# A two-layer conditioned trunk with a mixture of experts: additions of the rows read back placed further back, more PSUM banks for one-hot products, and two gating copies taken out

## The chip, the cores and the metric

The kernel runs on one core of one Trainium2 chip. The metric is the device time of one execution in microseconds (us). Before the change the median of three runs is 1160.93 us (1160.9 to 1163.3).

## What is computed

The reference runs two layers (DEPTH = 2) over 512 tokens of 1024 values. Each layer has a token mixer (three kinds of heads between an input and an output projection), and then a hierarchical mixture of experts: every token goes to 2 of 32 experts. The change lies in the second half:

```python
h = rms_norm(x, g_norm2[l]) * (1.0 + sc2) + sh2
x = x + ga2 * hier_moe(h, w_rg[l], b_rg[l], w_re[l], b_re[l], w1[l], w3[l], w2[l])
...
for g in range(N_GROUPS):                    # 4 groups of 8 experts, hidden width 256
    hid = jax.nn.silu(jnp.einsum('td,edf->tef', t, w1[g])) * jnp.einsum('td,edf->tef', t, w3[g])
    hid = hid * combine[:, g, :, None].astype(hid.dtype)   # zero but for a token's two experts
    y = y + jnp.einsum('tef,efd->td', hid, w2[g]).astype(jnp.float32)
```

## The kernel before

Everything is in float32; X is the running sum, four tiles of 128 tokens by 1024 (m = 0 to 3), kept in SBUF. SBUF is cut into 25 units of 1 MB (128 x 2048 values) that are handed out and given back in a queue.

**Experts in pairs.** The mixture runs over 16 pairs of experts. An expert's weights are three units: w1 and w3 by halves ("wg", two units, each loaded by two DMAs of 512 KB) and w2 (one unit, one DMA of 1024 KB), so a pair takes six units, 6 MB. Eighteen units hold weights, so up to three pairs are in SBUF. `pump` issues loads on SyncE's queue (SP), in order, as long as units are free; `refill` calls it again after a pair has released units. A DMA on that queue also waits until the one eight places before it has landed.

**One pair** (`pair(pr, b)`, b = pr % 2): the rows of up to 64 tokens of each of the two experts are gathered from DRAM (`gather`, an indirect DMA of GpSimd's queue, POOL) into xg, transposed (`rows_T`), multiplied with w1 and w3 (`stage1`, 32 records of L1118), made into the hidden values `hid` (ScalarE L1122, VectorE L1123), transposed (`hidden_T`, L1130 and L1131) and multiplied with w2 (`down`, L1138, two PSUM banks n = 0, 1). `extra` repeats this behind a branch when an expert has more than 64 tokens; it is taken at pair 0 and one later pair of layer 0, and at one pair of layer 1.

**Two ways back into X.** For pairs 0 to 12 `gated` multiplies with ga2 (L1153) and scatters the rows to y_d in DRAM. For the last three pairs (DIRECT = 3) the rows never leave the chip: `gated` (L1150) keeps them, `split` makes of them a high part yh (ScalarE L299) and a low part yl (VectorE L300), and `combine` adds them to X by a one-hot product: VectorE writes the 128 x 512 one-hot matrix `oh` (L1158), TensorE multiplies it with yh and yl into a PSUM bank per half tile (L1164, L1165), VectorE adds the bank to X (L1166). `combine` returns four steps, one per tile m; those of pair pr run inside `stage1` of pair pr + 1, after j = 2, 4, 6 and at its end; those of pair 15 run last of all. What was scattered is read back once (`fetch_back`, eight DMAs of 512 KB in pair 13) and added to X by `add_back(m)`, two VectorE additions of 128 x 1024 (L1208) per tile, in the tile order TAIL = (3, 0, 2, 1).

**Order.** In the last three pairs the order of TensorE, ScalarE, VectorE and GpSimd is that of the code (`manual_schedule(IN_LAST)`), before that only TensorE's and ScalarE's; SP is always in the order of the code. What belongs to the next layer (`front`) is placed between by a scheduler. Each engine works its own list in order, so an instruction that waits holds up all that stands behind it.

**The gate.** At the start of the mixture two gathers are issued, for pair 1 (xg[1]) and for the extra block of pair 0 (xg[2]). Then SP copies one value of each into a scrap of DRAM (L1218); since SP works in order, no load behind these copies starts before both gathers have landed. Behind them stand the two w2 loads of pair 2, and then everything from pair 3 on.

## Time and profile before

| | before |
|---|---|
| median of three runs | 1160.93 us |
| the profiled execution | 1162.47 us |
| its span, first to last instruction | 1160.5 us |
| TensorE busy | 1055.9 us (91%) |
| VectorE busy | 581.8 us (50%) |
| mean granted TensorE clock | 0.972 of full |

The mixture of layer 0 runs from about 318 to 602 us, that of layer 1 from about 880 us to the end. The page's 40 slices show the DMA engines 90% busy or more through most of both. Rows of a timeline are: start, duration, engine, line, operation, out<-in, tile, count, and in brackets how long the engine stood idle before and what ended it.

### The profile page before, as it was taken

The page shows a single profiled execution, that of the slowest core. Times are in us where ns is not written, and L with a number is a line of the kernel's source. Part 1 is how long each engine was busy: PE and PEld are TensorE (multiplying, and loading weights), DVE is VectorE, ACT ScalarE, POOL GpSimd, SP SyncE. Part 2 cuts the span into 40 slices and gives each one's busy share as a digit, 9 for nine tenths or more (in the row PEclk, how much of TensorE's full clock was granted, in tenths as well). Part 3 has the DMA queues.
Part 4 walks back from the last instruction along what each step waited for, and adds up shares of the span by engine and source line. Part 5 has one row for each costly group of instructions (what it writes and reads, how often), then busy time and mean ns, then how long its engine had stood idle before and what let it go on. Part 6 is the DMA issues. An engine that isn't in the chain of part 4 may idle for free. (4 is left out here: it accounts for less than half of the span.)

```text
span 1160.5 us, 15065 instructions
## 1 busy us (share of the span) xinstructions
PE 1055.9 (91%) x5152; PEld 571.9 (49%) x5152; DVE 581.8 (50%) x1315; ACT 359.4 (31%) x904; POOL 297.1 (26%) x260
## 2 busy tenths in 40 slices
PE   4999999999889999989779999999988998997975
PEld 1567666577533333333346676667763332332332
DVE  3567756778622222213584776587764221221255
ACT  2333354565311111201143333467632120120110
POOL 5655531002222221211134455110022221121100
PEclk9899999999999999999889999999989999999988
DMA  9957436816859999999976535620677999999992
GB/s 377 400 218 254 149 125 208 309 51 240 307 179 408 409 406 402 395 398 400 384 273 254 197 131 188 211 80 2 206 275 263 411 406 408 389 398 399 399 371 76
DMA packets 90909, 329.42 MB, mean 284 GB/s; under 512 B 19128, under 2 KB 23416, under 8 KB 76160
## 3 DMA queue, kind: packets, MB, share of 16 engines
q1 hardware_dynamic: 74992, 307.86, 69.6%
q0 software_dynamic: 14896, 17.50, 4.6%
q10 hardware_dynamic: 864, 2.17, 0.5%
q8 instruction: 74, 1.21, 0.4%
q14 instruction: 83, 0.68, 0.2%
HBM read 338.87 MB, written 29.93 MB: 318 GB/s over the span
## 5 line engine op out<-in xcount | busy, mean ns | idle before, releaser
L1118 PE MATMUL ps<-unit,unit 128*64 128x512 f32 x1120 | 271.5, 609 | 15.5 <-DMA unit<-w 14.8
L303 PE MATMUL ps<-unit,unit 128*128 128x512 f32 x448 | 182.6, 413 | 0.9 <-ACT unit L299 0.9
L304 PE MATMUL ps<-unit,unit 128*128 128x512 f32 x448 | 177.4, 397 | 2.8 <-POOL unit L300 1.5
L1118 PEld LDWEIGHTS ps<-unit,unit 128*64 128x64 f32 x1120 | 85.6, 140 | 186.0 <-issue 175.5
L305 PE MATMUL ps<-unit,unit 128*128 128x512 f32 x448 | 176.4, 396 | 0.5 <-DVE unit L300 0.5
L1138 PE MATMUL ps<-unit,unit 128*64 128x512 f32 x560 | 138.9, 618 | 6.5 <-ACT unit L1131 4.6
L1123 DVE SCALAR_TENSOR_TENSOR unit<-ps,slot_f,unit 128x256 f32<-128x256 f32 x35 | 16.9, 484 | 233.5 <-ACT unit L1122 233.5
L300 POOL TENSOR_TENSOR unit<-unit,unit 128x1024 fp32r<-128x1024 f32 (+1 forms) x46 | 104.9, 2284 | 100.9 <-ACT unit L299 100.9
L1122 ACT ACTIVATE unit<-ps 128x256 f32<-128x256 f32 x35 | 13.5, 384 | 371.5 <-issue 285.8
L299 ACT ACTIVATE unit<-unit 128x1024 fp32r<-128x1024 f32 (+1 forms) x92 | 87.9, 962 | 116.5 <-PE ps L305 60.8
L1087 POOL DMA_INDIRECT unit<-xn_d,slot_i x62 | 62.8, 1013 | 220.6 <-PEq L1186 160.9
L303 PEld LDWEIGHTS ps<-unit,unit 128*128 128x128 f32 x448 | 84.6, 189 | 36.6 <-issue 17.2
L304 PEld LDWEIGHTS ps<-unit,unit 128*128 128x128 f32 x448 | 84.9, 190 | 22.4 <-DVE unit L300 3.5
L305 PEld LDWEIGHTS ps<-unit,unit 128*128 128x128 f32 x448 | 84.3, 189 | 19.4 <-DVE unit L300 1.2
L1138 PEld LDWEIGHTS ps<-unit,unit 128*64 128x64 f32 x560 | 36.1, 139 | 82.8 <-issue 46.9
L1153 DVE TENSOR_TENSOR unit<-ps,unit 128x512 f32<-128x512 f32 x58 | 40.1, 692 | 72.1 <-PE ps L1138 72.1
L1092 POOL DMA_INDIRECT y_d<-unit,slot_y x29 | 29.6, 1021 | 171.2 <-DVE unit L1153 96.2
L535 ACT ACTIVATE unit<-unit,sm 128x512 f32<-128x512 f32 (+3 forms) x96 | 53.2, 555 | 32.9 <-DVE sm L533 32.4
L311 ACT ACTIVATE unit<-ps 128x512 f32<-128x512 f32 (+3 forms) x84 | 40.6, 490 | 70.6 <-PE ps L305 22.9
L1107 DVE TENSOR_SCALAR unit<-ps,cols 128x128 f32<-128x128 f32 x132 | 45.1, 404 | 31.4 <-PE ps L1098 31.1
L300 DVE TENSOR_TENSOR unit<-unit,unit 128x1024 fp32r<-128x1024 f32 (+1 forms) x46 | 54.9, 1198 | 11.7 <-ACT unit L299 11.1
L309 DVE COPY unit<-ps 128x512 f32<-128x512 f32 (+3 forms) x80 | 43.8, 552 | 31.8 <-PE ps L524 12.3
(223 smaller groups left out, 1346.0 us busy)
## 6 DMA issues: line engine op xcount, KB each, us to landing
unit<-w SPq DMA_DIRECT2D x256, 512.0 KB, 13.3
unit<-w SPq DMA_DIRECT2D x64, 1024.0 KB, 13.2
unit<-w_mod SPq DMA_DIRECT2D x48, 1024.0 KB, 7.0
unit<-w_in SPq DMA_DIRECT2D x16, 1024.0 KB, 14.9
y_d<-k_zero SPq DMA_DIRECT2D x16, 512.0 KB, 10.3
unit<-w_out SPq DMA_DIRECT2D x8, 1024.0 KB, 4.9
unit<-y_d SPq DMA_DIRECT2D x16, 512.0 KB, 10.7
unit<-w_in SPq DMA_DIRECT2D x8, 512.0 KB, 4.7
```

The costliest lines, as they stand in the source:

```text
L299: nc.scalar.activation(hi.bitcast(F32R), src, AF.Copy)
L300: (eng or nc.gpsimd).tensor_tensor(lo.bitcast(F32R), src, hi, op=OP.subtract)
L303: nc.tensor.matmul(o, ahi.bitcast(F32R), bhi.bitcast(F32R), start=first, stop=False)
L304: nc.tensor.matmul(o, ahi.bitcast(F32R), blo.bitcast(F32R), start=False, stop=False)
L305: nc.tensor.matmul(o, alo.bitcast(F32R), bhi.bitcast(F32R), start=False, stop=last)
L309: nc.vector.tensor_copy(dst, src)
L311: nc.scalar.activation(dst, src, AF.Copy)
L535: nc.scalar.activation(dst[:, :n], dst[:, :n], AF.Exp, bias=mx, scale=-1.0, accum_out=z)
L1087: nc.gpsimd.indirect_dma_start(out=dst, out_offset=None, in_=xn_d, in_offset=bass.IndirectOffsetOnAxis(ap=idx, axis=0), bounds_check=S - 1 ...
L1107: nc.vector.tensor_scalar(dst[:, j, :], p, cols[:, SC2, j:j + 1], cols[:, SH2, j:j + 1], op0=OP.mult, op1=OP.add)
L1118: nc.tensor.matmul(ph[64 * r:64 * r + 64, :], xT[:, j, 64 * r:64 * r + 64], ws[:, j % 4], start=j == 0, stop=j == 7, tile_position=(0, 64 ...
L1138: nc.tensor.matmul(PS[banks[n]][64 * r:64 * r + 64, :], hidT[b][:, j, 64 * r:64 * r + 64], w2[r][:, j, n, :], start=j == 0, stop=j == 1, t ...
```

## The change

It does three things. The two gate copies and their tile are taken out. In pair 15 the additions of the rows read back move: two tiles from the end of pair 14 into the second and third step of `combine` inside `stage1` of pair 15, the other two behind the one-hot matrix of the last `combine`, whose matrix is now written before `down` of pair 15 instead of after it. And the one-hot products inside `stage1` of pairs 14 and 15 use 4 and 6 PSUM banks instead of 2.

```diff
-    gate = dramp.tile([2, 1], F32, name="gate")
...
         TAIL = (3, 0, 2, 1)
+        tail = []
...
         gather(xg[2], slot_i[:, 0, 1:2])
-        for i, t in enumerate(xg[1:]):
-            nc.sync.dma_start(gate[i:i + 1, :], t[0:1, 0:1])
         pump()
 
         def pair(pr, b):
             tc.mark_branch_hint_location(f"extra{l}_{pr}", hint="LikelyTaken", engines=[mybir.EngineType.PE])
-            steps = combine(1 - b, slot_f[:, 0, pr - 1, 0:1], (6, 7)) if pr and direct(pr - 1) else []
+            steps = combine(1 - b, slot_f[:, 0, pr - 1, 0:1], (6, 7, 2, 3, 4, 5)[:6 if pr == 15 else 4]) if pr and direct(pr - 1) else []
             if pr == 15:
-                steps[1] = lambda s=steps[1]: (s(), add_back(TAIL[2]))
+                for k in (1, 2):
+                    steps[k] = lambda s=steps[k], m=TAIL[k - 1]: (s(), add_back(m))
             stage1(pr, b, xgT[b], slot_f[:, 1, pr, 0:1], steps)
...
                 hidden_T(b)
-                add_back(TAIL[3])
+                tail.extend(combine(b, slot_f[:, 0, pr, 0:1], (6, 7, 0, 4, 5, 1), done))
+                for m in TAIL[2:]:
+                    add_back(m)
             down(pr, b, each=lambda n: gated(pr, b, slot_y[:, pr, 0:1], n))
...
             refill(pr)
-            if pr == 14:
-                add_back(TAIL[0])
-                add_back(TAIL[1])
...
-            for f in combine(1, slot_f[:, 0, 15, 0:1], (6, 7, 0, 4, 5, 1), done):
+            for f in tail:
                 f()
```

VectorE, layer 1, from the end of pair 14 through `stage1` of pair 15 (unit_1 and unit_2 hold X; unit_339 and unit_336 are rows read back, tiles 3 and 0). Before:

```order
L300 TENSOR_TENSOR unit_335_10811<-ps_142,unit_334_10810 128x512
L1150 TENSOR_TENSOR ps_143<-ps_143,unit_3_172 128x512
L300 TENSOR_TENSOR unit_335_10811<-ps_143,unit_334_10810 128x512
L1208 TENSOR_TENSOR unit_2_171<-unit_2_171,unit_339_10815 128x1024 x2
L1208 TENSOR_TENSOR unit_1_170<-unit_1_170,unit_336_10812 128x1024 x2
L1158 TENSOR_SCALAR oh<-unit_3_172,slot_f 128x512
L1166 TENSOR_TENSOR unit_1_170<-unit_1_170,ps_146 128x512
```

After (line numbers are one or two lower):

```order
L299 TENSOR_TENSOR unit_335_10806<-ps_143,unit_334_10805 128x512
L1157 TENSOR_SCALAR oh<-unit_3_172,slot_f 128x512
L1165 TENSOR_TENSOR unit_1_170<-unit_1_170,ps_146 128x512
L1165 TENSOR_TENSOR unit_1_170<-unit_1_170,ps_147 128x512
L1165 TENSOR_TENSOR unit_1_170<-unit_1_170,ps_142 128x512
L1165 TENSOR_TENSOR unit_1_170<-unit_1_170,ps_143 128x512
L1208 TENSOR_TENSOR unit_2_171<-unit_2_171,unit_339_10810 128x1024 x2
L1165 TENSOR_TENSOR unit_2_171<-unit_2_171,ps_144 128x512
L1165 TENSOR_TENSOR unit_2_171<-unit_2_171,ps_145 128x512
L1208 TENSOR_TENSOR unit_1_170<-unit_1_170,unit_336_10807 128x1024 x2
L1122 SCALAR_TENSOR_TENSOR unit_258_8076<-ps_141,slot_f,unit_3_172 128x256
```

The matrix `oh` now stands right behind the last split; the four additions stand behind the additions of two products, and the last of them stands ahead of the hidden values (L1122).

VectorE, layer 0, behind the branch of pair 15, where the scheduler has placed work of layer 1's `front` (unit_195 receives lam_a and b_mod; unit_196 and unit_183 are a part of w_in). Before:

```order
L1208 TENSOR_TENSOR unit_1_170<-unit_1_170,unit_174_5155 128x1024 x2
L1150 TENSOR_TENSOR ps_142<-ps_142,unit_3_172 128x512
L300 TENSOR_TENSOR unit_172_5153<-ps_142,unit_171_5152 128x512
L1150 TENSOR_TENSOR ps_143<-ps_143,unit_3_172 128x512
L387 SCALAR_TENSOR_TENSOR unit_194_6001,lamt<-unit_195_6002 128x64 x2
L300 TENSOR_TENSOR unit_196_6003<-unit_183_5938,unit_196_6003 128x1024
L300 TENSOR_TENSOR unit_172_5153<-ps_143,unit_171_5152 128x512
L1158 TENSOR_SCALAR oh<-unit_3_172,slot_f 128x512
```

After:

```order
L1157 TENSOR_SCALAR oh<-unit_3_172,slot_f 128x512
L1208 TENSOR_TENSOR unit_2_171<-unit_2_171,unit_175_5153 128x1024
L250 MEMSET unit_195_5999 128x512
L1208 TENSOR_TENSOR unit_2_171<-unit_2_171,unit_175_5153 128x1024
L1208 TENSOR_TENSOR unit_1_170<-unit_1_170,unit_174_5152 128x1024
L250 MEMSET unit_195_5999 128x512
L1208 TENSOR_TENSOR unit_1_170<-unit_1_170,unit_174_5152 128x1024
L1149 TENSOR_TENSOR ps_142<-ps_142,unit_3_172 128x512
L386 SCALAR_TENSOR_TENSOR unit_194_5998,lamt<-unit_195_5999 128x64 x2
L299 TENSOR_TENSOR unit_196_6000<-unit_183_5933,unit_196_6000 128x1024
L299 TENSOR_TENSOR unit_172_5150<-ps_142,unit_171_5149 128x512
L1149 TENSOR_TENSOR ps_143<-ps_143,unit_3_172 128x512
```

Four additions and two memsets stand ahead of the first half of `gated` (L1149 on ps_142), and the two steps that read lam_a (L386) now stand between it and the split of that half.

GpSimd, layer 0, the loads of layer 1's small tables around the branch of pair 15. Before, ahead of the branch:

```order
L320 DMA unit_195_6002<-gk_a 128x64
L320 DMA unit_195_6002<-gq_a 128x64
L320 DMA unit_195_6002<-gq_c 128x64
L320 DMA unit_195_6002<-gk_c 128x64
L320 DMA unit_195_6002<-lam_a 128x256
L252 DMA unit_195_6002<-b_mod 4x512 x2
L1181 TENSOR_LOAD nblk
```

After, behind the branch:

```order
L319 DMA unit_195_5999<-lam_a 128x256
L408 DMA unit_189_5993<-k_rope 128x512
L373 DMA unit_189_5993<-k_band 128x1536
L251 DMA unit_195_5999<-b_mod 4x512
L379 TENSOR_TENSOR unit_198_6002<-unit_189_5993,unit_195_5999 128x256
```

The load of lam_a has moved from ahead of the branch to behind it; gk_a, gq_a, gq_c and gk_c stay ahead. All of them write into the unit that held the rows read back for tile 0, so they wait for `add_back(0)`.

## Rows read from the trace of the kernel before

**Rows 1.** The page's first line: span of the profiled execution.
```profile
span 1160.5 us, 15065 instructions
```
**Rows 2.** What SP's queue waited for, layer 1, 888 to 1112: us, times, longest.
```profile
SPq L158 <- DMA unit<-w: 159.0, 116, 3.6
```
**Rows 3.** The same view, layer 0, 340 to 566 us.
```profile
SPq L158 <- PEq L1188: 11.4, 1, 11.4
```
**Rows 4.** TensorE's timeline, layer 1, inside the mixture.
```profile
981.27 5.34 PE L1118 MATMUL ps<-unit,unit 128*64 128x512 f32 x14 [1.95 <-DMA unit<-w]
```
**Rows 5.** SP's timeline, layer 1, at the gate.
```profile
887.52 0.60 SPq L1218 DMA_DIRECT2D gate<-unit x2
888.23 24.97 SPq L158 DMA_DIRECT2D unit<-w  x19
```
**Rows 6.** Windows: stretch, length, busy by engine, clock, DMA share, GB/s; layer 1.
```profile
880.00:882.00 2.00, 2.00 (x11) 0.73 (x11) 2.00 (x10) 1.98 (x6) 0.00 (x0) 1.00 0.70 287
882.00:884.00 2.00, 2.00 (x12) 0.72 (x10) 0.20 (x1) 0.46 (x1) 1.00 (x1) 1.00 0.00 0
...
892.00:896.00 4.00, 4.00 (x20) 1.29 (x18) 1.34 (x2) 0.00 (x0) 1.31 (x2) 1.00 1.00 387
```
**Rows 7.** TensorE's timeline, layer 1, start of the mixture.
```profile
879.48 0.94 PE L1051 MATMUL ps<-unit 128*128 128x384 f32 x4
880.35 7.09 PE L1118 MATMUL ps<-unit,unit 128*64 128x512 f32 x32
...
893.45 7.04 PE L1118 MATMUL ps<-unit,unit 128*64 128x512 f32 x32
```
**Rows 8.** TensorE's timeline, layer 0, extra block of pair 0.
```profile
326.59 1.16 PE L1098 MATMUL ps<-ident,unit 128*128 128x128 f32 x8 [1.38 <-DMA unit<-xn_d,slot_i]
```
**Rows 9.** GpSimd's timeline, layer 0: issue of that block's gather.
```profile
322.26 1.02 POOL L1087 DMA_INDIRECT unit<-xn_d,slot_i  x1 [0.30 <-issue]
```
**Rows 10.** The gathers' line: issue to landing over all 62.
```profile
DMA to landing us min/median/max: 3.2/7.6/10.0
```
**Rows 11.** VectorE's timeline, layer 1, pairs 14 and 15.
```profile
1118.79 0.69 DVE L300 TENSOR_TENSOR unit<-ps,unit 128x512 fp32r<-128x512 f32 x1 [0.72 <-ACT unit L299]
1120.22 5.07 DVE L1208 TENSOR_TENSOR unit<-unit,unit 128x1024 f32<-128x1024 f32 x4 [0.74 <-DMA unit<-y_d]
...
1145.17 0.70 DVE L1150 TENSOR_TENSOR ps<-ps,unit 128x512 f32<-128x512 f32 x1 [4.71 <-PE ps L1138]
...
1148.85 0.69 DVE L300 TENSOR_TENSOR unit<-ps,unit 128x512 fp32r<-128x512 f32 x1 [0.72 <-ACT unit L299]
...
1153.01 3.68 DVE L1166 TENSOR_TENSOR unit<-unit,ps 128x512 f32<-128x512 f32 x6 [0.17 <-PE ps L1165]
```
**Rows 12.** TensorE's timeline, layer 1, pair 15.
```profile
1125.84 0.77 PE L1164 MATMUL ps<-unit,oh 128*128 128x512 f32 x1 [6.25 <-DVE oh L1158]
...
1130.24 0.49 PE L1164 MATMUL ps<-unit,oh 128*128 128x512 f32 x1
...
1133.24 0.50 PE L1164 MATMUL ps<-unit,oh 128*128 128x512 f32 x1
...
1140.20 0.46 PE L1130 MATMUL ps<-ident,unit 128*128 128x128 f32 x1 [3.34 <-PEq L1186]
```
**Rows 13.** Windows, layer 1, pair 15; the clock is the third number from the end.
```profile
1123.00:1128.00 5.00, 2.17 (x6) 1.35 (x8) 3.33 (x5) 0.00 (x0) 0.00 (x0) 0.50 1.00 411
```
**Rows 14.** VectorE's timeline, layer 0, pairs 14 and 15.
```profile
567.12 0.69 DVE L300 TENSOR_TENSOR unit<-ps,unit 128x512 fp32r<-128x512 f32 x1 [0.72 <-ACT unit L299]
...
593.60 0.68 DVE L300 TENSOR_TENSOR unit<-ps,unit 128x512 fp32r<-128x512 f32 x1
594.20 0.50 DVE L1158 TENSOR_SCALAR oh<-unit,slot_f 128x512 fp32r<-128x512 f32 x1
```
**Rows 15.** DMA issues by transfer: count, KB each, us to landing.
```profile
unit<-lam_a POOLq DMA_DIRECT2D x1, 128.0 KB, 8.7
unit<-gk_a POOLq DMA_DIRECT2D x1, 32.0 KB, 6.0
```

## The prediction

> **What bounds the kernel now.** The span is 1160.5 us [rows 1]; the profiled execution took 1162.47 us, 1.5 us above the median of the runs shown (1160.93). I make the sum in the span's time and take it off the median. The change touches three places, and I read each by what ends the waits there.
>
> First, the mixture of layer 1. From 888 to 1112 us SP's queue waits 159 us in 116 pieces for an earlier weight load to land, and for hardly anything else [rows 2]: the loads run back to back, and no wait for a free unit is visible beside that. TensorE waits for weights in the pairs of that stretch ([rows 4] is one of seven such stalls). So from 888 us on, the stream of weights sets the time, and a stream that is ahead by some microseconds ends the stage as much earlier. Second, the start of this stream: SP stands at the gate until 887.52 and issues the two w2 loads of pair 2 at 888.23 [rows 5], while the DMA engines are idle: their work runs out inside 880 to 882, and from 882 to 884 they move nothing [rows 6]. Third, the end of layer 1: after the last split of pair 14 VectorE makes four additions, 5.07 us, behind a wait of 0.74 us for the rows read back [rows 11], and only then the one-hot matrix; TensorE stands idle for 6.25 us for it [rows 12].
>
> Layer 0 has the same code and other limits. At its start SP stands 11.4 us for the end of pair 0's extra block [rows 3], whose weights' units it needs; the two w2 loads lie ahead of that wait either way. At its end the scheduler has woven in work of layer 1.
>
> **Layer 1, gate out: -5.8 us.** Removed are two small DMAs; moved are two loads of 1024 KB and, behind them, the whole stream. The units that the two loads fill are free when the last product of the router ends, at 879.48 + 0.94 = 880.42 [rows 7], so they issue at about 880.5 and run in the idle stretch: 2.10 MB at 387 GB/s [rows 6] is 5.4 us, from about 882 to 887.5. The next load, of pair 3, needs the units of pair 0, free when stage1 ends at 880.35 + 7.09 = 887.44 [rows 7], so it now issues at 887.5 where the first w2 load did at 888.23 [rows 5]: 0.7 us. Before, pair 3 had to queue behind those 5.4 us. Together 6.1 us; I take 5.8, as the gathers share the idle stretch. Nothing needs these two loads before pair 2, so what hides them is stage1 of pair 0. Does the lead last to the end? It is lost where loads come to wait for units; pair 4's loads ask for the units of pair 1, free when its stage1 ends at 893.45 + 7.04 = 900.5 [rows 7], and the DMA engines are busy with pair 3 (six units, 6.3 MB at 387 GB/s, 16 us) until about 905, so no. Low end 3.0 us, if half the loads are pushed past 888; high end 6.1.
>
> **Layer 0, gate out: +1.5 us.** There the same move frees nothing, since the stream goes on only when the extra block ends. But the loads now run while the gathers do. TensorE already waits 1.38 us for the extra block's rows, until 326.59 [rows 8]; that gather was issued at 322.26 [rows 9], 4.3 us before. Gathers under the stream take 7.6 us in the median [rows 10], so the delay lies between 0 and 3.3 us. The loads, started near 320, are gone by about 326, so only part of the gather is under load: I take 1.5, and it passes to all of layer 0, for both TensorE and the stream start from the end of that block. In layer 1 the gather for pair 1 may be late by as much, but there TensorE is behind the stream later anyway and the delay is absorbed.
>
> The Trainium skill ("DMA: Bandwidth & Descriptors", Queues, rings and completion order) says that each DMA engine goes round between the queues it has work for, a packet at a time. By that a gather has no right of way over weights, which speaks for the gate; it is the second rival below.
>
> **Layer 1, the tail: -7.6 us.** The matrix now starts when the last split ends, 1118.79 + 0.69 = 1119.48 [rows 11]; before, the additions ended at 1125.29 and the product began at 1125.84 [rows 11, 12]. The first product so begins at about 1120.1, 5.7 us earlier. The clock gives back more: after its idle stretch TensorE was granted half speed (1.2 GHz) from 1123 to 1128 [rows 13]; from the first product to the second took 1130.24 - 1125.84 = 4.40 us, from the second to the third, with equal work, 3.00 [rows 12]. Without the idle stretch I take 3.00: 1.4 us. TensorE's stage1 is then 7.1 us early, and the 3.34 us at the branch [rows 12], which no engine's work explains, stay.
>
> The additions have not gone; VectorE must still make all eight (1.24 us each, 5.07/4 less overlap [rows 11]) ahead of `gated`. From the second product's bank, at about 1123.9, it makes without a pause: six half additions from PSUM (0.61 each [rows 11], 3.7), the hidden values (0.5), the branch (0.3), the matrix (0.5) and eight additions (9.9), in all 14.9, so it is ready for `gated` at 1138.8. `down` has its first half at 1145.17 - 7.1 = 1138.1 [rows 11]. So 0.7 of the 7.1 is lost, and `hid`, now behind an addition, costs nothing on top, since VectorE is what is late. `gated` then goes through in 4.2 us as before (1145.17 to 1149.54 was 4.37): the last split ends 6.5 us early. Behind it the matrix (0.5) no longer stands, and the first product needs the first half alone: from the last split to the last addition were 1156.69 - 1149.54 = 7.15 us [rows 11]; now eight halves of 0.61 and one wait of about 1.1, 6.0. Sum: 6.5 + 1.1 = 7.6. Bounds: 8.4 if no wait is left; 5.0 if the clock stays low and the last products are waited for as before. The additional PSUM banks free the fourth step from the second's additions, worth some tenths at most; I count 0.
>
> **Layer 0, the tail: -0.4 us.** The same move starts the matrix right after 567.12 + 0.69 [rows 14], but its gain meets two things. VectorE has four additions and two memsets ahead of `gated`, so it begins that at about 588 and not 7 us early. And the two lam_a steps now stand between `gated` and its split, with lam_a's load behind the branch. gk_a waits for the additions of tile 0, which end near 579.6 (567.8, plus 0.6 to the product, two steps of 3.0, and the halves and additions behind); its three followers take GpSimd to 582, the branch to about 584. A load of this kind lands 6.0 to 8.7 us after its issue [rows 15], so lam_a lands between 588 and 592.7, against VectorE's 588.6. Behind it stand 0.5 + 1.2 + 0.7 + 0.7 + 0.6 + 0.7 = 4.4 us to the end of the last split. With lam_a at 590.4, in the middle, that is 594.8, against 593.60 + 0.68 = 594.28 before [rows 14]; 0.5 us late, less the matrix (0.4) and part of the first product (0.5) that no longer follow. So -0.4, between -2.4 (lam_a in time) and +1.7.
>
> **Sum:** -5.8 + 1.5 - 7.6 - 0.4 = -12.3 us: 1162.47 to 1150.2 for the profiled execution, 1148.6 on the median. Best ends together: -16.9; worst: -3.0.
>
> **Rivals.**
> 1. *The lead of the loads is not carried* (TensorE becomes the bound before the end, or the stream waits for units): for it, TensorE runs several pairs after layer 1's extra block without a stall; against it, it stalls again after them, and SP's waits name only loads [rows 2]. Without the 5.8: 1154.4. Chance 0.12.
> 2. *The gathers pay for the gate*, as the round between the queues has it: each takes its 3.3 us in both layers, and in layer 1 the stream loses as much of its lead. For it, [rows 10]; against it, the loads end while the gathers run. 1148.6 + 1.8 + 3.3 = 1153.7. Chance 0.15.
> 3. *VectorE takes back most of the tail*, clock and last products as before: layer 1's tail -5.0 and layer 0's +1.7: 1153.3. Chance 0.07.
> 4. *lam_a comes in time and the gathers are not disturbed*: 1148.6 - 2.0 - 1.5 = 1145.1. Chance 0.06.
> 5. *Slower*: VectorE, working in order, stands in layer 0 for lam_a with all of `gated` and the last additions to X behind it, and layer 1 cannot start. It costs a microsecond for each that lam_a lands after 590.4, and the whole turns slower when it lands after about 590.4 + 12.3 = 602.7, 19 us after its issue, against 8.7 measured at most: 1162 and more. Chance 0.03.
> 6. *Nothing arrives at the end* (the gains cancel with stalls that I don't see): 1161. Chance 0.04.
>
> **How the numbers follow.** The forecast, 1148.6, has 0.53. The range from 1144.5 to 1155.0 takes in rivals 1 to 4 and leaves out 5, 6 and the worst ends. About 0.2% (2.3 us) is what a measurement of this kernel can tell from no change: faster 0.93 (forecast and rivals 1 to 4), same 0.04, slower 0.03.
>
> **What would show it.** Right: SP issues the w2 loads of pair 2 near 881 in layer 1 and the next ones near 887.5 (each less what layer 0 moved), with the stalls for weights in the later pairs as long as before; TensorE idle under 1 us ahead of the first one-hot product of pair 15, at full clock; eight additions of L1208's kind ahead of `gated`; in layer 0 a wait of 0 to 4 us at the lam_a steps, and the extra block's gather 0 to 3.3 us later. Wrong: stalls for weights gone from layer 1's later pairs (the lead not carried); a half-speed stretch in pair 15's first products; lam_a landing later than 9 us after issue.

## The result, and the profile after

The changed kernel takes 1149.36 us (median of four, 1146.0 to 1149.47) against 1162.12 us of the kernel before (1160.9 to 1165.18): a ratio of 0.9875, 95% interval 0.9849 to 0.9901. The prediction was 1148.6 us, from 1144.5 to 1155.0. Executions of one kernel spread over some 8 us here, so single profiles differ by a microsecond or two where nothing was changed.

The total was right: 12.3 us were forecast, and 12.8 lie between the medians (14.5 by the ratio, and 16.6 by the ratio when the kernel was measured again). The experiments below show that its terms were not: the gate is worth about nothing in all, and what it was to bring came, as far as the runs show, from the PSUM banks, which I had counted at 0. First the places of [rows 1 to 15] in the changed kernel; timeline rows are start, duration, engine, line, operation, tiles, count, and in brackets the idle time before with what ended it.

The span, answering [rows 1]:

```profile
span 1147.4 us, 15064 instructions
```

**Layer 0, the extra block of pair 0** ([rows 8, 9]). GpSimd issues its gather, TensorE waits for it:

```profile
321.92 1.02 POOL L1086 DMA_INDIRECT unit<-xn_d,slot_i  x1 [0.30 <-issue]
...
329.77 1.97 PE L1097 MATMUL ps<-ident,unit 128*128 128x128 f32 x8 [4.89 <-DMA unit<-xn_d,slot_i]
331.67 7.88 PE L1117 MATMUL ps<-unit,unit 128*64 128x512 f32 x32
...
345.94 0.70 PE L1097 MATMUL ps<-ident,unit 128*128 128x128 f32 x4 [0.61 <-PEq L1187]
```

Windows of the same stretch, before and then after (busy by engine; the last three numbers are the granted clock, the DMA share and GB/s):

```profile
322.00:326.00 4.00, 3.21 (x16) 0.86 (x12) 0.26 (x1) 0.38 (x1) 2.01 (x2) 1.00 0.48 119
```
```profile
322.00:326.00 4.00, 2.88 (x14) 0.72 (x10) 0.48 (x1) 0.38 (x1) 1.93 (x2) 1.00 1.00 395
326.00:328.00 2.00, 0.00 (x0) 0.00 (x0) 0.00 (x0) 0.00 (x0) 0.00 (x0) 1.00 0.69 261
328.00:332.00 4.00, 2.23 (x10) 1.87 (x12) 0.22 (x1) 1.01 (x3) 0.00 (x0) 0.74 0.07 28
```

The gather took 329.77 - 321.92 = 7.85 us, against 4.3 before. From 322 to 326 us the DMA engines moved 395 GB/s, the weights among it, against 119 before. And TensorE, idle for 4.89 us, came back at a lower clock: 1.97 us for the eight transposes that took 1.16, 7.88 for a stage1 of 7.09. The first product behind the block starts at 345.94; before it was

```profile
341.31 0.70 PE L1098 MATMUL ps<-ident,unit 128*128 128x128 f32 x4 [0.54 <-PEq L1188]
```

so layer 0 is 4.6 us late there.

**Layer 1, the stream of weights.** What SP's queue waited for from 879 to 1108 us, to be held against [rows 2], and TensorE at pair 1, against [rows 7]:

```profile
SPq L157 <- DMA unit<-w: 135.1, 98, 4.0
SPq L157 <- PEq L1185: 13.5, 4, 5.2
SPq L157 <- PE ps L1137: 4.2, 4, 3.4
```
```profile
891.38 0.71 PE L1097 MATMUL ps<-ident,unit 128*128 128x128 f32 x4 [2.81 <-DMA unit<-xn_d,slot_i]
...
898.08 7.04 PE L1117 MATMUL ps<-unit,unit 128*64 128x512 f32 x32
```

A wait that was not there before: 13.5 us in four pieces for TensorE to pass a branch (L1185), that is for units to come free. 5.2 us of it is the wait for pair 0 that I expected; 8.0 us lie between 895 and 930 us.

**Layer 1, the tail** ([rows 11, 12]), VectorE and then TensorE:

```profile
1114.98 0.69 DVE L299 TENSOR_TENSOR unit<-ps,unit 128x512 fp32r<-128x512 f32 x1 [0.72 <-ACT unit L298]
1115.59 0.48 DVE L1157 TENSOR_SCALAR oh<-unit,slot_f 128x512 fp32r<-128x512 f32 x1
...
1127.14 0.48 DVE L1122 SCALAR_TENSOR_TENSOR unit<-ps,slot_f,unit 128x256 f32<-128x256 f32 x1
...
1129.43 4.87 DVE L1208 TENSOR_TENSOR unit<-unit,unit 128x1024 f32<-128x1024 f32 x4
1134.22 0.69 DVE L1149 TENSOR_TENSOR ps<-ps,unit 128x512 f32<-128x512 f32 x1
...
1142.28 1.88 DVE L1165 TENSOR_TENSOR unit<-unit,ps 128x512 f32<-128x512 f32 x3 [0.17 <-PE ps L1164]
```
```profile
1116.21 0.47 PE L1163 MATMUL ps<-unit,oh 128*128 128x512 f32 x1 [0.43 <-DVE oh L1157]
...
1127.67 0.39 PE L1129 MATMUL ps<-ident,unit 128*128 128x128 f32 x1 [2.16 <-DVE unit L1122]
```

The matrix stands right behind the last split, TensorE waits 0.43 us for it instead of 6.25. From the end of the last split of pair 14 (1115.67) to the end of the last addition (1144.16) are 28.5 us, against 37.2 before (1119.48 to 1156.69): 8.7 less. VectorE passes from the additions (L1208) to `gated` (L1149) without a pause: it is what is late. The 3.34 us at the branch of [rows 12] are gone, and in their place is a wait of 2.16 us for the hidden values.

### The profile page after: what moved, and what is told of

It is laid out like the page before. It is cut to its first block, busy times and chain, and to the rows that moved or that the text cites. A ratio compares the mean times of both kernels' runs of the same rounds, so it can differ in the third digit from the quotient of the medians.

```text
span 1147.4 us, 15064 instructions
## 1 busy us (share of the span) xinstructions
PE 1052.2 (92%) x5152; PEld 569.8 (50%) x5152; DVE 581.2 (51%) x1315; ACT 360.5 (31%) x905; POOL 297.3 (26%) x260
## 3 DMA queue, kind: packets, MB, share of 16 engines
q10 hardware_dynamic: 864, 2.17, 0.5%
## 5 line engine op out<-in xcount | busy, mean ns | idle before, releaser
L1117 PE MATMUL ps<-unit,unit 128*64 128x512 f32 x1120 | 261.1, 599 | 11.3 <-DMA unit<-w 10.8
L1137 PE MATMUL ps<-unit,unit 128*64 128x512 f32 x560 | 143.7, 630 | 5.7 <-ACT unit L1130 1.9
L1122 DVE SCALAR_TENSOR_TENSOR unit<-ps,slot_f,unit 128x256 f32<-128x256 f32 x35 | 16.9, 484 | 224.0 <-ACT unit L1121 224.0
L1121 ACT ACTIVATE unit<-ps 128x256 f32<-128x256 f32 x35 | 13.4, 384 | 347.6 <-issue 277.9
L1097 PE MATMUL ps<-ident,unit 128*128 128x128 f32 x264 | 44.3, 295 | 21.6 <-PEq L1185 12.2
```

Source lines behind the costliest of these rows:

```text
L1097: nc.tensor.transpose(PS[banks[j // 4]][:, 128 * (j % 4):128 * (j % 4) + 128], v[:, j, :], ident)
L1117: nc.tensor.matmul(ph[64 * r:64 * r + 64, :], xT[:, j, 64 * r:64 * r + 64], ws[:, j % 4], start=j == 0, stop=j == 7, tile_position=(0, 64 ...
L1137: nc.tensor.matmul(PS[banks[n]][64 * r:64 * r + 64, :], hidT[b][:, j, 64 * r:64 * r + 64], w2[r][:, j, n, :], start=j == 0, stop=j == 1, t ...
```

## The experiments

All were timed beside the kernel before; ratios are to it, with 95% intervals, and "us" is the ratio's distance from 1 times 1162.

| kernel | median us | ratio | us |
|---|---|---|---|
| gate out alone | 1164.48 | 1.0009 [0.9991, 1.0026] | +1 |
| banks alone | 1155.42 | 0.9932 [0.9907, 0.9956] | -8 |
| additions moved alone | 1152.28 | 0.9904 [0.9883, 0.9925] | -11 |
| additions moved and banks (gate kept) | 1147.40 | 0.9885 [0.9856, 0.9915] | -13 |
| additions moved and gate out (two banks) | 1153.11 | 0.9917 [0.9899, 0.9935] | -10 |
| all three: the changed kernel, again | 1146.87 | 0.9857 [0.9828, 0.9886] | -17 |
| all, gate put back in layer 0 | 1144.63 | 0.9859 [0.9837, 0.9880] | -16 |
| the same, hidden values first | 1143.17 | 0.9831 [0.9801, 0.9862] | -20 |

The time of each layer's mixture in the profiled executions, in us, worked out from the traces. It runs from the first record of stage1 on TensorE's weight-load queue (a wait that stands 1.7 us ahead of the first load) to the end of the last addition of a product:

| kernel | layer 0 | layer 1 |
|---|---|---|
| before | 285.7 | 278.0 |
| gate out alone | 289.2 | 277.3 |
| banks alone | 282.7 | 272.9 |
| additions moved alone | 285.4 | 268.5 |
| additions moved and banks | 282.2 | 267.6 |
| additions moved and gate out | 292.2 | 264.3 |
| all three; again | 286.6; 288.4 | 264.4; 265.2 |
| all, gate put back in layer 0 | 282.1 | 265.4 |
| the same, hidden values first | 281.7 | 264.5 |

These are single profiles. Up to pair 14 of each layer the four kernels with the gate in both layers (before, banks, moves, both) have the same code, and their pair 14 starts, counted from the layer's first product, up to 1.3 us apart in layer 0 and 1.9 us in layer 1. Between the two mixtures, where nothing was changed, the profiles of the table took 274.9 to 279.3 us. So a difference of one or two us in this table is not shown by it alone.

**Gate out alone.**

```diff
-    gate = dramp.tile([2, 1], F32, name="gate")
...
-        for i, t in enumerate(xg[1:]):
-            nc.sync.dma_start(gate[i:i + 1, :], t[0:1, 0:1])
```

> The kernel before with nothing changed but the gate copies taken out. My theory (the stream of weights is ahead by some 5 us in layer 1 and keeps it; in layer 0 the extra block's gather is slower): layer 1 gains 4.5 to 6 us up to the end of pair 14, layer 0 loses some 1 to 2 us by its end although it is 4 to 5 us late after pair 0, so 2.5 to 5 us faster than before. Rival (the gathers pay for the gate in both layers, the lead is lost): within 1 us of before. Rival (the gate is worth nothing, the whole change is the tail): equal to before, and the later pairs of layer 1 start when they did.

Measured: no difference that can be told from zero, 1.0009. Layer 0 loses 3.5 us, layer 1 gains 0.7. The lead of the loads was there and shrank: counted from the DMA records, of all queues together and mostly weights, the first 4, 16, 40 and 88 MB after the start of layer 1's stage1 had moved 18.2, 49.9, 111.7 and 238.7 us behind it before, and 12.3, 45.5, 107.3 and 235.5 us without the gate: 5.9 us ahead, then 4.4, 4.4, 3.2. My theory falls for the size in both layers; the rival that the gathers pay for the gate gives the total.

**Additions moved and banks, gate kept.**

```diff
+        for i, t in enumerate(xg[1:]):
+            nc.sync.dma_start(gate[i:i + 1, :], t[0:1, 0:1])
         pump()
```

> The changed kernel with the two gate copies put back: only the moved additions and the banks are left. My theory: the tail of layer 1 is worth 8 to 9 us and that of layer 0 between 0 and 2 us, so 8 to 10 us faster than before and 2.5 to 5 us slower than the changed kernel. Rival (the gate carries most of it): less than 5 us faster than before. In the trace the extra block of layer 0 starts after a wait of about 1.4 us again, and TensorE's idle time ahead of the first one-hot product of pair 15 in layer 1 stays under 1 us.

Measured: 13 us faster than before, more than the 8 to 10 that I expected, and as much as the whole change within the intervals; so it is not the 2.5 to 5 us slower than the changed kernel that I had written. The extra block of layer 0 waits 1.63 us again, and layer 0 is 3.5 us shorter than before where I had given its tail 0.4.

**All three, the gate in layer 0 alone.**

```diff
+        for i, t in enumerate(xg[1:] if l == 0 else []):
+            nc.sync.dma_start(gate[i:i + 1, :], t[0:1, 0:1])
```

> The changed kernel with the gate copies put back in layer 0 alone. My theory: the extra block of layer 0 waits 1.4 us and not 4.9 us, TensorE is 4.6 us earlier after pair 0, of which 1 to 2 us are left at the end of layer 0, since the stream of weights bounds its later pairs; layer 1 keeps its gain: 0.5 to 2.5 us faster than the changed kernel. Rival (the w2 loads that ran early in layer 0 were a lead that the later pairs use): 0 to 2 us slower than the changed kernel, with longer stalls for weights in the later pairs of layer 0.

Measured: layer 0 takes 282.1 us, 4.5 less than in the changed kernel, layer 1 within 1 us of it. TensorE's wait at the extra block is 0.58 us. In time it is 2.2 us faster than the changed kernel by the two medians (1144.63, 1146.87), and equal to it by the ratios to the runs of before beside each (0.9859, 0.9857), so a difference isn't shown by the times. The rival that the early loads are a lead for layer 0 is out: the layer got shorter.

**All three, with two banks.**

```diff
-(6, 7, 2, 3, 4, 5)[:6 if pr == 15 else 4]
+(6, 7)
```

> The changed kernel with two banks (6 and 7) again for the one-hot products in stage1 of pairs 14 and 15. My theory: the steps of pair 15 wait for VectorE's additions, which now stand between the products, so TensorE in pair 15's stage1 loses up to 1 us per step from the third on; in pair 14 nothing. But VectorE is what is late behind it, so 0 to 1.5 us slower than the changed kernel. Rival (banks carry the tail): over 3 us slower.

Measured: 1153.11, some 4 to 6 us slower than the changed kernel: what the rival says, and over my bound. Layer 1 is as short as with the banks (264.3); layer 0 is 4 to 6 us longer. Where, the trace says: `down` of pair 14 stood still in its first products for 2.52 us, for "issue". The kernel before has the same stall, the kernels with more banks don't. Before, additions moved alone, and banks alone:

```profile
561.76 3.16 PE L1138 MATMUL ps<-unit,unit 128*64 128x512 f32 x13 [1.88 <-issue]
```
```profile
560.51 4.86 PE L1138 MATMUL ps<-unit,unit 128*64 128x512 f32 x13 [2.42 <-issue]
```
```profile
558.11 4.04 PE L1138 MATMUL ps<-unit,unit 128*64 128x512 f32 x16
```

**The changed kernel again**, so that the next ones have it beside them.

> The changed kernel, unchanged, beside the same runs of the kernel before as the next three. Expected: 12 to 15 us faster than before, between the kernel with the gate kept in both layers (1147.4) and the one with two banks (1153.1); the layer-0 gate in alone was 1144.6, so it should be 1 to 5 us slower than that. If it is as fast as 1145, the loss that I put on layer 0's gathers is not there.

Measured: 1146.87 us (1143.42 to 1149.51), 0.9857, 17 us faster than before (13 to 20) where I had expected 12 to 15; the wait at the extra block of layer 0 was 3.18 us here.

**Banks alone.**

```diff
-combine(1 - b, slot_f[:, 0, pr - 1, 0:1], (6, 7))
+combine(1 - b, slot_f[:, 0, pr - 1, 0:1], (6, 7, 2, 3, 4, 5)[:6 if pr == 15 else 4])
```

> The kernel before with nothing changed but the banks of the one-hot products in stage1 of pairs 14 and 15 (4 and 6 in place of 2). My new theory: with two banks TensorE's queue stands at the last product of the stage until VectorE has emptied a bank, and reaches the branch behind it late, so that what follows the branch is waited for with nothing else to run (3.3 us in pair 15 of layer 1, 1.9 us in pair 14 of layer 0, seen in the three kernels with two banks and in none of the others). With more banks the branch is reached while products still run: 2 to 5 us faster than before, the 3.34 us at the branch of layer 1's pair 15 under 1 us, no stall of 1.9 us in `down` of layer 0's pair 14. Rival (what I wrote in the prediction, banks worth some tenths): within 1 us of before, with the stalls where they were.

Measured: 8 us faster (5 to 11), more than the 2 to 5 that I expected even then. The branch in pair 15 of layer 1, on TensorE's queue (PEldq; duration in ns thrice, then its start): before, banks alone, and the changed kernel:

```profile
L1186 PEldq COMPARE_BRANCH  x1: 3417/3417/3417, 1136.5 to 1136.5; - x1
```
```profile
L1186 PEldq COMPARE_BRANCH  x1: 3688/3688/3688, 1131.6 to 1131.6; - x1
```
```profile
L1185 PEldq COMPARE_BRANCH  x1: 4701/4701/4701, 1120.8 to 1120.8; - x1
```

The branch takes 3.4 to 4.7 us in the three of them. What differs is when TensorE's queue gets to it. TensorE with two banks, before (the row left out is the 1140.20 of [rows 12], idle for 3.34 us):

```profile
1136.47 0.39 PE L1165 MATMUL ps<-unit,oh 128*128 128x512 f32 x1
...
1141.02 0.49 PE L1130 MATMUL ps<-ident,unit 128*128 128x128 f32 x1 [0.37 <-ACT unit L1131]
1141.44 5.93 PE L1138 MATMUL ps<-unit,unit 128*64 128x512 f32 x16
```

and with the banks alone:

```profile
1136.01 0.39 PE L1165 MATMUL ps<-unit,oh 128*128 128x512 f32 x1
1136.55 0.36 PE L1130 MATMUL ps<-ident,unit 128*128 128x128 f32 x1
1137.28 0.39 PE L1130 MATMUL ps<-ident,unit 128*128 128x128 f32 x1 [0.37 <-ACT unit L1131]
1137.59 3.65 PE L1138 MATMUL ps<-unit,unit 128*64 128x512 f32 x16
```

Before, the last product waits until VectorE has emptied its bank, and the branch behind it begins at 1136.5, with the last product itself: its 3.4 us lie bare. With more banks it begins at 1131.6, 4.8 us ahead of the end of the products (1136.01 + 0.39); they run on, and 0.15 us is left. The idle time had a second price: `down` took 5.93 us after it and 3.65 without it. The granted clock, third from the end, in that stretch before, and then with the banks alone:

```profile
1140.00:1147.00 7.00, 6.43 (x18) 2.01 (x18) 1.57 (x3) 1.15 (x3) 0.00 (x0) 0.57 0.01 2
```
```profile
1136.50:1141.00 4.50, 4.08 (x18) 1.45 (x18) 4.06 (x5) 0.65 (x3) 0.00 (x0) 1.00 0.01 2
```

Together that is 3.3 + 2.3 us, of which VectorE, late itself, lets 5.1 through to the end of layer 1.

During the branch the DMA queue named "instruction" is at work, and in the kernel before it has the engines to itself. All queues that moved anything there from 1134 to 1142 us, with packets, MB and share:

```profile
q8 instruction: 2, 0.03, 1.7%
q14 instruction: 1, 0.01, 0.4%
```

The Trainium skill ("Runtime: NRT & Kernel Launch", Instruction fetch mechanics) says that a taken branch to a place outside the fetched pages must wait for a DMA of the target page. The trace agrees: in every kernel of this document a transfer of 16 KB on that queue lies inside this branch, in the kernel before from 1137.57 to 1138.60 of 1136.55 to 1139.97.

**Other banks for the fourth step alone.**

```diff
-combine(1 - b, slot_f[:, 0, pr - 1, 0:1], (6, 7))
+combine(1 - b, slot_f[:, 0, pr - 1, 0:1], (6, 7, 6, 7, 6, 7, 2, 3))
```

> The kernel before with other banks for the fourth step's products alone (2 and 3; the first three steps keep 6 and 7). My theory: what costs with two banks is only that the last products, for which VectorE must first empty a bank, hold TensorE's queue ahead of the branch; so this alone brings nearly all that the banks brought: 5 to 9 us faster than before, the branch in pair 15 of layer 1 reached some 3 us ahead of the end of the products and its idle time under 1 us. Rival (the products of the earlier steps wait for banks): under 3 us faster, the 3.34 us still there.

Measured: 1157.04, 0.9962 [0.9945, 0.9979], 4.4 us faster. The branch begins at 1131.58, 3.6 us ahead of the end of the products (1134.79 + 0.39), and its idle time is gone, as is the stall in `down` of layer 0's pair 14:

```profile
L1186 PEldq COMPARE_BRANCH  x1: 2662/2662/2662, 1131.6 to 1131.6; - x1
```

So the mechanism at the branch is that of the last step. In layer 0 it is in part argued: the branch of pair 14 itself took 0.33 us there, and that the 1.88 us of "issue" in the kernel before are the wait for a page rests on a transfer of 16 KB just ahead of them (559.26 to 560.16). The time is under what I wrote. Whether the first three steps' banks bring the 3.5 us that are missing to the kernel with all banks, the times don't show: the two intervals overlap, and the profiles of the two have the same span (1154.5 and 1154.6 us). By the profiles layer 1 is 1.8 us longer than with all banks, and there the clock differs: the eight products of stage1 behind the first step of pair 15 took 3.68 us against 2.75, at a granted clock of 0.50 and 0.61 in the stretches around them, and from the first of the last products to the end of the last addition were 7.5 us against 6.4, at 0.50 and 0.65.

**Additions moved alone.**

```diff
+        for i, t in enumerate(xg[1:]):
+            nc.sync.dma_start(gate[i:i + 1, :], t[0:1, 0:1])
...
-(6, 7, 2, 3, 4, 5)[:6 if pr == 15 else 4]
+(6, 7)
```

(against the changed kernel)

> The kernel before with the moved additions alone: gate kept, two banks. With the banks alone (7.9 us faster) and both (13.3) this closes the square. My theory: the two share a gain, since with the additions moved TensorE waits for the hidden values behind an addition in any case, and the time at the branch lies beside that wait: 8 to 11 us faster than before, with the idle 3.3 to 3.6 us at layer 1's branch and the 1.9 to 2.5 us in `down` of layer 0's pair 14 still in the trace. Rival (the two add up): 13.3 - 7.9 = 5.4 us faster.

Measured: 11 us faster (9 to 14). With the banks' 8 that would be 19, and both together are 13 (10 to 17): they share a gain, as expected: 5.7 us by the ratios, whose intervals allow much less, and 4 us by the layers' table. In layer 1 the branch's 3.35 us lie in part beside a wait for VectorE that is there anyway. TensorE, and VectorE's hidden values:

```profile
1130.94 0.46 PE L1130 MATMUL ps<-ident,unit 128*128 128x128 f32 x1 [3.18 <-DVE unit L1166]
```
```profile
1129.28 0.48 DVE L1123 SCALAR_TENSOR_TENSOR unit<-ps,slot_f,unit 128x256 f32<-128x256 f32 x1
```

The hidden values are ready at 1129.76, the branch ends at 1130.78. With the banks as well this wait is 2.17 us, so on top of the moved additions they bring 1 us in layer 1, and 3.2 us in layer 0.

**GpSimd adds the last two tiles, early.**

```diff
...
             if pr == 15:
+                for m in TAIL[2:]:
+                    add_back(m, nc.gpsimd)
...
-                for m in TAIL[2:]:
-                    add_back(m)
```

> The kernel with the gate in layer 0 alone (1144.6), and the additions of the last two tiles read back made by GpSimd at the start of pair 15 in place of VectorE behind the matrix. My theory (VectorE is what is late ahead of `gated`): GpSimd needs about 2.45 us for each of the four, 9.8 us, beside stage1; VectorE has 4.9 us less to do ahead of `gated`, which then waits for `down`: 2 to 3 us earlier in layer 1, 0 to 2 us in layer 0, so 2 to 4 us faster than 1144.6. Rival (TensorE sets the tail): within 1 us of it. Rival (GpSimd's additions hold up VectorE's, or step three waits for them): 1 to 3 us slower than it.

Measured: 1160.21, 14 us (by the ratios) to 16 us (by the medians) slower than with VectorE. It is a wait for GpSimd, as in my second rival, but at a price far over its 1 to 3 us, and at the second step. GpSimd and then VectorE:

```profile
1121.65 9.52 POOL L1209 TENSOR_TENSOR unit<-unit,unit 128x1024 f32<-128x1024 f32 x4 [12.89 <-DMA unit<-y_d]
```
```profile
1131.21 1.28 DVE L1166 TENSOR_TENSOR unit<-unit,ps 128x512 f32<-128x512 f32 x2 [12.94 <-POOL unit L1209]
```

The rows of these tiles are read back last and land at 1121.65; the second step's additions to the same tile stand behind GpSimd's.

**Hidden values first** (on the kernel with the gate in layer 0).

```diff
-                for k in (1, 2):
-                    steps[k] = lambda s=steps[k], m=TAIL[k - 1]: (s(), add_back(m))
+                for k, m in ((1, TAIL[0]), (3, TAIL[1])):
+                    steps[k] = lambda s=steps[k], m=m: (s(), add_back(m))
```

> The kernel with the gate in layer 0 alone (1144.6), with the second tile's additions in pair 15 behind the fourth step and so behind the hidden values, not ahead of them. My theory: TensorE's wait of 2.16 us for the hidden values goes, `down` is 2 us earlier, but VectorE has as much to do ahead of `gated` as before, so within 1 us of 1144.6 (in layer 0 the loads that wait for this tile come later by 2 us, which may cost 0 to 2 us). Rival (the hidden values behind an addition cost their whole wait): 2 to 4 us faster than 1144.6.

Measured: 1143.17, 1.5 us under the kernel that it starts from by the medians and 3 us by the ratios, within the intervals. The wait for the hidden values is gone (0.70 us at the branch is left), and VectorE still goes from the additions to `gated` without a pause; in layer 0 `down` now waits for its weights:

```profile
579.07 1.89 PE L1138 MATMUL ps<-unit,unit 128*64 128x512 f32 x2 [2.72 <-DMA unit<-w]
```
```profile
1123.47 4.87 DVE L1209 TENSOR_TENSOR unit<-unit,unit 128x1024 f32<-128x1024 f32 x4
1128.26 0.69 DVE L1150 TENSOR_TENSOR ps<-ps,unit 128x512 f32<-128x512 f32 x1
```

It is the fastest median of all; that it beats the changed kernel (0.9831 against 0.9857 beside the same runs of before) the intervals don't show.

**GpSimd adds the last tile, or the last two in layer 1, late** (on the kernel just above).

```diff
...
                 for m in TAIL[2:]:
-                    add_back(m)
+                    add_back(m, nc.gpsimd if m == TAIL[3] else nc.vector)
```

The second has `if l or m == TAIL[3]` there, and takes the tiles in the other order.

> The kernel with the gate in layer 0 alone and the hidden values ahead of the second tile (1143.2), with the two additions of the last tile given to GpSimd where they stand, behind the last matrix. They wait for nothing that the earlier try waited for: the tile's own products of pair 15 are done by then. My theory (VectorE sets the start of `gated`): VectorE has 2.4 us less ahead of it, so 1 to 3 us faster than 1143.2, both layers together, with `gated` waiting for `down`. Rival (the w2 loads, for which `down` waits now, set it): within 1 us. Rival (lam_a, now behind 4.9 us of additions on GpSimd, is late in layer 0): 0 to 3 us slower.

> The same with both last tiles on GpSimd in layer 1 (9.8 us there) and one in layer 0. My theory: in layer 1 VectorE has 4.9 us less ahead of `gated`, but `down` ends its first half only about 2.5 us before the present start of `gated`, and GpSimd must be done before the last products' additions: within 1 us of the kernel with one tile on GpSimd. Rival (VectorE's share counts in full): 2 us faster than that. Rival (the rows read back land late and GpSimd ends behind the products): 1 to 3 us slower than it.

Measured: 1150.63 (0.9901 [0.9877, 0.9925]) and 1146.98 (0.9865 [0.9843, 0.9887]), both with a median over that without (1143.17, 0.9831); for the second the intervals overlap. Between the two the second is the faster by 4 us, nearest to its rival of VectorE's share. Two causes show, in the first of them, GpSimd, VectorE and TensorE:

```profile
1125.31 4.83 POOL L1209 TENSOR_TENSOR unit<-unit,unit 128x1024 f32<-128x1024 f32 x2 [20.39 <-DVEq L1186]
```
```profile
1125.38 2.56 DVE L1158 TENSOR_SCALAR oh<-unit,slot_f 128x512 fp32r<-128x512 f32 x1 [0.22 <-DVEq L1186]
1127.86 4.63 DVE L1209 TENSOR_TENSOR unit<-unit,unit 128x1024 f32<-128x1024 f32 x2
```
```profile
1126.39 6.18 PE L1138 MATMUL ps<-unit,unit 128*64 128x512 f32 x14 [1.22 <-DMA unit<-w]
```

While GpSimd adds, VectorE's matrix takes 2.56 us for 0.49, and its two additions 4.63 for 2.48: the 2.4 us given away come back as 4.2 us. And `down` waits for its weights. This accounts for no gain. Why the first loses 7 us in the median stays open: its profiled execution is its fastest of six and only some 4 us behind, and these 4 us lie between the mixtures (279.3 us against 275.0), where nothing was changed; the two mixtures together take 546.3 us against 546.2.

## Why the total was right and its terms were not

By layers the forecast was close: +1.1 in layer 0 and -13.4 in layer 1, measured (286.6 - 285.7, 264.4 - 278.0) +0.9 and -13.6. By its own terms, each from the layers' table:

| term | predicted | measured |
|---|---|---|
| layer 1, gate out | -5.8 (-3.0 to -6.1) | -3.2 (-0.7 to -4.2) |
| layer 0, gate out | +1.5 (0 to +3.3) | +4.4 (+3.5 to +6.8) |
| layer 1, additions moved | -7.6 (-5.0 to -8.4) | -9.5 |
| layer 0, additions moved | -0.4 (-2.4 to +1.7) | -0.3 |
| banks, both layers | 0 | -4.1 on top of the moves, -8.1 alone |

(Measured values: the gate's from the changed kernel against the one with the gate kept, in brackets the other three pairs with and without it; the moves from additions moved alone; the banks from there to both.) By these single profiles the gate was forecast 5.5 us too good, banks and moves 5.9 us too small. They cancel; the sum held by luck. The ratios say the same of the gate with less precision: with and without it they differ by -3 to +1.5 us in four pairs of kernels, each within its intervals, where -4.3 was forecast. One slip of the sum itself is small: from lam_a at 588.6 and 592.7 the bounds of layer 0's tail come out as -2.2 and +1.9, not -2.4 and +1.7.

**The gate, layer 1.** With the gate out alone the lead arises as worked out, 5.9 us at the first 4 MB; in the changed kernel, against the one with the gate kept, it is 3.7 us there (5.2 in the second profile). The step that failed is "does the lead last": I let pair 4's loads ask for the units of pair 1 at 900.5 and find the DMA engines busy until about 905. But the gather for pair 1 was late as well, and TensorE with it by 2.81 us, so pair 1's stage1 ended at 898.08 + 7.04 = 905.1, and SP waited for units, the 8.0 us between 895 and 930. I had called that delay absorbed because TensorE is behind the stream later anyway; it is, but the units that it frees late feed the stream. What these waits cost isn't shown: in each 5 us from 894 to 929 the DMA engines were still busy (shares of 1.01 to 1.05), and the lead of the changed kernel went only from 3.7 us at 4 MB to 3.4 at 16 and 3.1 at 88. The engines had less to do earlier, behind the two w2 loads, where SP stood for pair 0:

```profile
889.00:894.00 5.00, 2.62 (x14) 1.48 (x14) 1.78 (x5) 1.76 (x7) 1.44 (x2) 0.91 0.79 217
```

In the kernel before the same stretch has 341 GB/s at a share of 0.95. So about half of what rival 1 takes away was lost, and its mechanism, a stream that waits for units, is seen in SP's waits but not measured as the cause.

With the gate out alone, layer 1 ends only 0.7 us shorter, though 3.2 us of lead are left at 88 MB. The two profiles show where most of that went: in pair 13 TensorE waits longer for weights and comes back at a lower clock. Before, and then with the gate out, TensorE and the window of the same products:

```profile
1087.17 3.62 PE L1118 MATMUL ps<-unit,unit 128*64 128x512 f32 x14 [0.87 <-DMA unit<-w]
```
```profile
1087.00:1090.80 3.80, 3.62 (x14) 1.19 (x14) 0.00 (x0) 0.00 (x0) 0.00 (x0) 1.00 1.02 412
```
```profile
1088.23 6.61 PE L1117 MATMUL ps<-unit,unit 128*64 128x512 f32 x14 [3.87 <-DMA unit<-w]
```
```profile
1088.20:1094.90 6.70, 6.61 (x14) 1.70 (x14) 0.00 (x0) 0.00 (x0) 0.00 (x0) 0.55 0.97 381
```

Counted from the first load of stage1 of the layer (880.35 and 883.55), these weights come 2.1 us earlier, and the fourteen products take 3.0 us longer. The end of pair 14's last split is then 1.2 us ahead.

**The gate, layer 0.** Two sizes. The gather's delay is 3.5 us in the first profile, a little over the upper bound (1.8 in the second profile of the changed kernel and with the gate out alone, where the gather took 6.1 us), not the 1.5 of a gather only partly under load: the window from 326 to 328 us is still 0.69 full. And the idle stretch had a price in clock, 0.8 us each for the transposes and stage1 (in the other two, 1.7 us in stage1 alone, 8.78 for 7.09), which I had reckoned with in layer 1's tail and not here. Rival 2 is what happened to the gate: it puts +3.3 us in layer 0 and -2.5 in layer 1, against +4.4 and -3.2 in the table. The Trainium skill ("DMA: Bandwidth & Descriptors", Queues, rings and completion order) has the engines going round between queues packet by packet. The trace agrees in that the gather has no right of way, with 4.3 us behind the gate and 7.85 beside the weights; the going round itself no run shows.

**Banks.** The step that failed is the sentence "The additional PSUM banks free the fourth step from the second's additions, worth some tenths at most; I count 0", together with the 3.34 us at the branch, "which no engine's work explains", that were to stay. They are one thing. The fourth step's wait is short, but it stands ahead of a branch in TensorE's queue, and the branch costs 3.4 us from when the queue gets there. In layer 0 the stall that goes with the banks is "issue" in `down` of pair 14, 1.88 us, which the prediction doesn't have.

**Additions moved.** Right in mechanism and nearly in size. VectorE needed 14.3 us from the second product's bank to `gated` (1119.95 to 1134.22 in the changed kernel), worked out as 14.9; the tail behind the last split took 5.8 us in the changed kernel, where I had 6.0, and 4.9 with the additions moved alone, all eight halves without a pause. "`hid`, now behind an addition, costs nothing on top" holds: putting it first took TensorE's wait away and left `gated` where VectorE is ready. In layer 0 lam_a landed about 6.9 us after its issue, at 592.7, the late end of what I gave it, since layer 0 ran late as a whole; VectorE waited for it:

```profile
592.77 0.23 DVE L386 SCALAR_TENSOR_TENSOR unit<-unit 128x64 f32<-128x64 f32 x1 [2.28 <-DMA unit<-lam_a]
```

**What would show it.** Right: the idle time ahead of the first product and its clock (1.00 from 1116 to 1127 us), eight additions ahead of `gated`, lam_a's wait of 0 to 4 us, and SP's w2 loads at 881.59 and the next at 888.71, both some 1.1 us behind the 880.5 and 887.5 of the sum, as much as layer 1 starts later. Of the signs that I gave for wrong, stalls for weights did not vanish from layer 1's later pairs but shrank, from 10.2 us in seven to 6.1 in four between 880 and 1112 us.

## What to carry to other kernels

Where an engine's queue stands at a wait just ahead of a branch, the price can be the whole branch and the clock after it, as here, and not the wait: give the last instructions ahead of a branch buffers of their own, so that the queue gets past it while work still runs. A wait that seems to waste a transfer's time can be what keeps a short, urgent transfer clear of long ones; take it out only where the lead of the long ones is worth more than the wait for the short one. By the profiles that is so here in layer 1 and not in layer 0; the times of the two kernels don't differ clearly. A sum that comes out right proves none of its terms: one kernel for each part, and one for each pair of parts that may share a gain.

## What the runs showed of the hardware that I had not expected

GpSimd held VectorE up when both added from SBUF: two VectorE additions of 128x1024 took 4.63 us instead of 2.48, and the one-hot matrix 2.56 instead of 0.49. GpSimd's own additions took as long as without VectorE beside them: two took 4.83 us, and four took 9.52 where they stood early and VectorE waited for them. The Trainium skill ("SBUF — State Buffer", Who interferes with whom) says so for VectorE instructions with two SBUF inputs against GpSimd ones that read SBUF; the trace agrees for the additions. The matrix reads one tile and a scalar, which that sentence doesn't cover.

The branch at pair 15 of layer 1 took 2.7 to 3.7 us on TensorE's queue in the six kernels where it fell behind the weight stream (the DMA engines 0 to 28% busy), and 4.7 to 6.1 us in the eight where it fell into its end (74 to 88% busy).
